# First mixer of a two-layer decoder: where the norm squares, the rotary sum and the decays stand in their engines' order

## The chip, the cores and the metric

The kernel runs on one core of one Trainium2 chip. The metric is device microseconds (us) of one execution; the time before is 1045.48 us, the median of 3 runs that lie between 1041.57 and 1046.89 us.

## The reference

The program is the trunk of a two-layer hybrid decoder on 256 tokens with a model width of 1024. Each layer adds half a SwiGLU feed-forward, a mixer and another half feed-forward to the residual. The mixer of the first layer, the only place that the change touches, joins two kinds of heads that read the same normalized input:

```python
x += 1/2 SwiGLU(RMSNorm(x)); x += W_out[SSD heads | MLA heads](RMSNorm(x)); x += 1/2 SwiGLU(RMSNorm(x))

# MLA heads: low-rank q and kv, RMSNorm on both, rotary part of 32, causal softmax over blocks of 128 rows
p = jax.nn.softmax(where(causal, einsum("bqhd,bkhd->bhqk", q, k) * scale, -inf))
# SSD heads: convolution and SiLU of x, B, C; dt = softplus(...); decays from the cumulated a = dt * A
y_diag = einsum("bclgn,bcsgn,bcgels,bcgesp->bclgep", C, B, exp(segsum(a)), x * dt)
```

The softmax of the MLA heads and the decays exp(segsum(a)) of the SSD heads do not depend on each other. The kernel keeps both at float32 accuracy: it splits every operand into a high and a low part and makes three products of each matrix product.

## The kernel before

All weights come through one stream. For every piece of a weight, `Stream.load` issues a DMA on SyncE into one of 4 raw buffers, has ScalarE cast it to the high part `wh` (L77), and VectorE subtract that to give the low part `wl` (L78). A raw buffer comes free once both have read it. TensorE then multiplies `wh` with the high and the low part of the activations and `wl` with the high part. The pieces are in the order of the program, so a mixer's weights are cast while TensorE still works on what stands before them.

The order in which each engine issues its instructions is made when the program is built: a scheduler takes the program's dependences and a model of durations and lays out a list for each engine. Engines then run their lists in order, so an instruction that waits holds everything behind it on that engine. `order(later, earlier)` adds one more constraint to the scheduler, that `later` stands behind `earlier` in the lists; on one engine it costs no semaphore.

The first mixer, `mixer0` (L461 to L765), runs over two tiles of 128 tokens (t = 0, 1):

- The low-rank products `p_qa` (400 wide: 16 for dt, 384 for q) and `p_kva` (288 wide) go to PSUM. ScalarE squares and sums them into `ssn` (L481, L482, L484) and copies the rotary part of k into `pe` (L483). VectorE adds epsilon (L485), GpSimd takes the power of -1/2 (L234, in `power`), VectorE scales with it into `qn` (L488, L489). TensorE turns `qn` (L117, `m_qaT` and `m_kvT`), and the turned tile is split in high and low again (L229, L230).
- `xbc(c)` makes one of 16 channel tiles of the convolution: 24 matmuls into a PSUM bank (L294 to L296), then `conv_silu`: one ScalarE instruction (L442) and three of VectorE (L444) read the bank, ScalarE's tanh (L447) and a VectorE instruction (L448) finish it. B and C come first (8 tiles), x behind (8 tiles); they are TensorE's work while the rest is prepared. The banks of all projections (`p_xbc`, `p_qb`, `p_kvb`) are 4 in turn.
- The q projection `p_qb` (from L516): for each token tile two halves of 4 heads, 9 matmuls each. ScalarE squares each half (L526) and copies it in two parts (L528, L529), VectorE sums the squares (L527), GpSimd rotates the last 32 columns in five instructions, four products (L457, L458) and their sum (L459), and takes the power for the scale of q (L234 on `sqs`). TensorE turns the result (`m_qT`).
- The kv projection `p_kvb`, with the same steps for k (`knat`, L559 to L564).
- Softplus of dt by `log1p_exp` (L389): ScalarE's Abs (L393) and Exp (L394), a polynomial on VectorE. Its cumulated sum goes to DRAM as `acs_rows` (L592) and comes back spread over all partitions as the E tiles (L648).
- `softmax(t)` (L604): scores on TensorE (`m_sc`), row maximum on VectorE (L617), 8 exponentials of ScalarE with their sums (L622), reciprocal (L419) and, on GpSimd, the product with it (L420); then TensorE turns the probabilities (`m_pT`).
- `decays(t)` (L638): for each of 4 groups of 4 heads 4 Relus (L654) and one Exp (L657) of ScalarE on E, a copy on GpSimd (L659, t = 0 only), and a product with `cb` on VectorE (L660).

What bound the decays to a place in ScalarE's list before is one line: the first Relu of t = 0 stands behind the last tanh of the convolution tiles before it.

Of the kernel before, what the change touches and what calls it, by code (L numbers as in the profile page):

```python
# [11 lines left out]
AF = mybir.ActivationFunctionType  # L12
ALU = mybir.AluOpType
# [43 lines left out]
class Stream:  # L57
# [10 lines left out]
    def load(self, widths):  # L68
        nc = self.nc
        res = []  # L70
        for i, x in enumerate(widths):
            raw = self.pool.tile([P, x], F32, tag="raw", name=f"raw{self.n}_{i}", bufs=self.raw_bufs)
            nc.sync.dma_start(out=raw, in_=self.flat[self.off:self.off + P * x].rearrange("(p w) -> p w", w=x))
            self.off += P * x
            hi = self.pool.tile([P, x], F32R, tag="wh", name=f"wh{self.n}_{i}", bufs=self.bufs)
            lo = self.pool.tile([P, x], F32R, tag="wl", name=f"wl{self.n}_{i}", bufs=self.bufs)
            nc.scalar.copy(out=hi, in_=raw)  # L77
            nc.vector.tensor_tensor(out=lo, in0=raw, in1=hi.bitcast(F32), op=ALU.subtract)  # L78
            res.append((hi, lo))
        self.n += 1  # L80
        return res


class Net:
# [302 lines left out]
        self.proj(NF, at, x, 0.5, after)  # L387


    def log1p_exp(self, v, e, name):  # L390

        nc = self.nc
        nc.scalar.activation(out=e, in_=v, func=AF.Abs)  # L393
        nc.scalar.activation(out=e, in_=e, func=AF.Exp, scale=-1.0)  # L394
        acc = self.blk(list(v.shape), name)
        nc.vector.tensor_scalar(out=acc, in0=e, scalar1=LOG1P[-1], scalar2=None, op0=ALU.mult)
        for c in LOG1P[-2::-1]:
            nc.vector.scalar_tensor_tensor(out=acc, in0=acc, scalar=c, in1=e, op0=ALU.add, op1=ALU.mult)
        return acc
# [50 lines left out]
    def apply_rope(self, out, x, t, which, nh):  # L450

        nc = self.nc
        cg, sg = self.rope[which]
        tmp = self.small([P, nh, 2, 16], f"rtmp{nh}")
        for h in range(2):
            shape = [P, nh, 16]
            nc.gpsimd.tensor_tensor(out=out[:, :, h, :], in0=x[:, :, h, :], in1=cg[:, t, h:h + 1, :].broadcast_to(shape), op=ALU.mult)  # L457
            nc.gpsimd.tensor_tensor(out=tmp[:, :, h, :], in0=x[:, :, 1 - h, :], in1=sg[:, t, h:h + 1, :].broadcast_to(shape), op=ALU.mult)  # L458
        nc.gpsimd.tensor_tensor(out=out, in0=out, in1=tmp, op=ALU.add)  # L459

    def mixer0(self, hT, x, after):  # L461
        nc, st, row = self.nc, self.st, self.row
# [5 lines left out]
        dtv = self.small([P, 2, 16], "dtv")  # L468
# [5 lines left out]
        for t in range(2):  # L474
            c = slice(t * P, (t + 1) * P)
            pq, pk = self.bank([P, 400], "qa"), self.bank([P, 288], "kva")
            self.in_tok(pq, hT, t, w1, 400, 2)
            self.in_tok(pk, hT, t, w2, 288, 2)
            nc.vector.tensor_tensor(out=dtv[:, t, :], in0=pq[:, :16], in1=row[:, ROW["dt_bias"]], op=ALU.add)
            junk = self.small([P, 512], "junk")  # L480
            nc.scalar.activation(out=junk[:, :384], in_=pq[:, 16:], func=AF.Square, scale=384.0 ** -0.5, accum_out=ssn[:, t, 0:1])  # L481
            nc.scalar.activation(out=junk[:, :256], in_=pk[:, :256], func=AF.Square, scale=1.0 / 16, accum_out=ssn[:, t, 1:2])  # L482
            nc.scalar.copy(out=pe[:, t, :], in_=pk[:, 256:])  # L483
            nc.scalar.activation(out=junk[:, :32], in_=pk[:, 256:], func=AF.Square, accum_out=ssn[:, t, 2:3])  # L484
            nc.vector.tensor_scalar(out=ssn[:, t, 0:2], in0=ssn[:, t, 0:2], scalar1=EPS, scalar2=None, op0=ALU.add)  # L485
            self.power(rsn[:, t, :], ssn[:, t, 0:2])
            qn = self.blk([P, 640], "qn", grp="a")
            nc.vector.scalar_tensor_tensor(out=qn[:, :384], in0=pq[:, 16:], scalar=rsn[:, t, 0:1], in1=row[:, ROW["q_a"]], op0=ALU.mult, op1=ALU.mult)  # L488
            nc.vector.scalar_tensor_tensor(out=qn[:, 384:], in0=pk[:, :256], scalar=rsn[:, t, 1:2], in1=row[:, ROW["kv_a"]], op0=ALU.mult, op1=ALU.mult)  # L489
            tp = self.tbank([P, 3, P], "qaT", "a")  # L490
            for j in range(3):
                self.transpose(tp[:, j, :], qn[:, j * P:(j + 1) * P])
            self.split(qaT[0][:, :, c], qaT[1][:, :, c], tp)
            tp = self.tbank([P, 2, P], "kvT", "a")
            for j in range(2):
                self.transpose(tp[:, j, :], qn[:, (3 + j) * P:(4 + j) * P])
            self.split(kvT[:, 0, :, c], kvT[:, 1, :, c], tp)
# [9 lines left out]
        for i in range(4):  # L507
            xbc(8 + i, BC[0][:, i, :])

        wq = st.load([768, 768]) + st.load([768])  # L510
        V = self.blk([P, 2, 8, 64], "V", grp="a")
        qT = [self.blk([96, 8, P], f"qT{t}", grp="a") for t in range(2)]
        kT = [self.blk([96, 8, P], f"kT{t}", grp="a") for t in range(2)]
# [1 line left out]
        for t in range(2):  # L515
            qn = self.blk([P, 8, 96], "qnat", grp="a")  # L516
            qr = self.blk([P, 8, 2, 16], "qr")
            for j in range(2):
                b = self.bank([P, 4, 96], "qb")
                bf = b.rearrange("p a b -> p (a b)")  # L520
                for k in range(3):
                    self.mm_tok(bf, lambda k: (qaT[0][:, k, :], qaT[1][:, k, :]), [k], t,
                                [(wq[k][0][:, j * 384:(j + 1) * 384], wq[k][1][:, j * 384:(j + 1) * 384])], k == 0, k == 2)
                hs = slice(4 * j, 4 * j + 4)
                junk = self.small([P, 512], "junk")[:, :384].rearrange("p (a b) -> p a b", a=4)
                nc.scalar.activation(out=junk, in_=b, func=AF.Square)  # L526
                nc.vector.tensor_reduce(out=sq[:, t, hs], in_=junk, op=ALU.add, axis=X)  # L527
                nc.scalar.copy(out=qn[:, hs, :64], in_=b[:, :, :64])  # L528
                nc.scalar.copy(out=qr[:, hs, :, :], in_=b[:, :, 64:].rearrange("p a (s d) -> p a s d", s=2))  # L529
            self.apply_rope(qn[:, :, 64:].rearrange("p a (s d) -> p a s d", s=2), qr, t, "q", 8)  # L530

            nc.vector.tensor_scalar(out=sq[:, t, :], in0=sq[:, t, :], scalar1=96 * EPS, scalar2=None, op0=ALU.add)
            self.power(sq[:, t, :], sq[:, t, :])
            for j in range(2):
                tp = self.tbank([96, 4, P], "qT", "a")
                for i in range(4):
                    self.transpose(tp[:, i, :], qn[:, 4 * j + i, :])
                nc.scalar.copy(out=qT[t][:, 4 * j:4 * j + 4, :], in_=tp)
# [32 lines left out]


        e = self.small([P, 2, 16], "dte")
        l1 = self.log1p_exp(dtv, e, "dtl")
        dts = self.edge.tile([P, 2, 16], F32, tag="dts", name="dts", bufs=1)
        nc.vector.scalar_tensor_tensor(out=dts, in0=dtv, scalar=0.0, in1=l1, op0=ALU.max, op1=ALU.add)
        ea = self.small([P, 16], "ea")
# [26 lines left out]
        def softmax(t):  # L604
# [3 lines left out]
            for j in range(8 // n):  # L608
# [10 lines left out]
                for i in range(n):  # L619
                    h = n * j + i  # L620
                    m = 8 // (t + 1)
                    nc.scalar.activation(out=pr[h // m][:, h % m, :], in_=b[:, i, :], func=AF.Exp, scale=sq[:, t, h:h + 1],  # L622
                                         bias=mx[:, t, h:h + 1], accum_out=den[:, t, h:h + 1])
                m = 8 // (t + 1)
                h = n * j
                self.normalize(pr[h // m][:, h % m:h % m + n, :], den[:, t, hs])
            for kb in range(t + 1):
                PT[t, kb] = self.turn_probs(lambda h: pr[h // m][:, h % m, kb * P:(kb + 1) * P], kb, f"pT{t}{kb}")
        oT = [self.blk([P, 2, 4, P], f"oT{t}", F32R, grp="a") for t in range(2)]
        for t in range(2):  # L630
            softmax(t)
            self.attend(t, lambda b, h: PT[t, b][:, h, :], lambda b, h: V[:, b, h, :],
                        (oT[t][:, 0], oT[t][:, 1]))

# [3 lines left out]
        def decays(t):  # L638
# [10 lines left out]
            for g in range(4):  # L649
                eb = E[g // 2][:, 4 * (g % 2):4 * (g % 2) + 4, :]  # L650

                for i in range(4):
                    h = t * 16 + 4 * g + i
                    first = nc.scalar.activation(out=eb[:, i, :], in_=eb[:, i, :], func=AF.Relu, scale=-1.0, bias=acs[:, h:h + 1])  # L654
                    if t == g == i == 0:
                        self.order(first, self.tanh)
                nc.scalar.activation(out=eb, in_=eb, func=AF.Exp, scale=-1.0)  # L657
                if t == 0:
                    nc.gpsimd.tensor_copy(out=dec[:, 4 * g:4 * g + 4].unsqueeze(2), in_=eb[:, :, P - 1:P])  # L659
                nc.vector.tensor_tensor(out=eb, in0=eb, in1=cb[:, g:g + 1, :].broadcast_to([P, 4, P]), op=ALU.mult)  # L660
# [504 lines left out]
```

## Time and profile before

| | |
|---|---|
| median of 3 runs | 1045.48 us (1041.57 to 1046.89) |
| the profiled execution | 1043.0 us, span 1041.2 us |
| mean granted TensorE clock | 0.993 |
| TensorE busy (matmul) | 1012.2 us, 97% of the span |
| VectorE, ScalarE, GpSimd busy | 687.4 us (66%), 569.6 us (55%), 86.5 us (8%) |
| DMA | 185.95 MB, mean 179 GB/s |
| chain that ended last | TensorE 92%, ScalarE 2%, DMA 2%, VectorE 2% |

The first mixer lies between about 205 and 333 us of the span. In the profile, a row of a timeline gives the start, the duration, the engine, the line and the operation, output and inputs by the names of the program, how many instructions the row joins, and in brackets the idle time before it with the instruction that ended it. The granted clock of 1.00 is 2.4 GHz, and 0.50 is 1.2 GHz.

### The profile page before, as it was taken

Reading aid. Unit: us, or ns where it says so; the run is one execution under the profiler, and the core shown is the slowest. Engines: PE = TensorE matmul, PEld = TensorE weight load, DVE = VectorE, ACT = ScalarE, POOL = GpSimd, SP = SyncE. Lnnn points to the kernel's source line nnn. Section 1 sums busy time; section 2 is a strip of 40 time slices with the busy share of each in tenths; the row PEclk is TensorE's granted clock in tenths of the full one; section 3 lists DMA queues with packets and bytes.
Section 4 is the critical chain, followed back from the end, with each engine's and each line's share of the span. In section 5 each row is a group of like instructions: output and inputs, shape, how many; then the busy total and the mean of one; then the engine's idle time right before and its main releaser. Section 6 shows DMA issues by size and latency. Waiting matters only on the chain.

```text
span 1041.2 us, 15138 instructions
## 1 busy us (share of the span) xinstructions
PE 1012.2 (97%) x5609; PEld 867.8 (83%) x5609; DVE 687.4 (66%) x1056; ACT 569.6 (55%) x1036; POOL 86.5 (8%) x110
## 2 busy tenths in 40 slices
PE   6999999989799999999999999999999899999998
PEld 5888888888788888888888888888887678888886
DVE  6887654588777667676546776654588576666541
ACT  5665643477767366656434655543466356555530
POOL 2100000006233200000000000000012200000000
PEclk9999999999899999999999999999999899999999
DMA  8875556364434457555564655655463355655451
GB/s 292 273 220 186 190 194 176 116 223 153 158 102 161 144 182 244 194 189 185 198 191 155 229 195 185 194 188 165 142 222 101 103 162 183 190 192 182 150 195 41
DMA packets 52090, 185.95 MB, mean 179 GB/s; under 512 B 5911, under 2 KB 5928, under 8 KB 52016
## 3 DMA queue, kind: packets, MB, share of 16 engines
q1 hardware_dynamic: 49248, 176.58, 51.7%
q0 software_dynamic: 2048, 6.83, 2.0%
q10 hardware_dynamic: 720, 1.57, 0.4%
q8 instruction: 44, 0.72, 0.3%
q14 instruction: 30, 0.25, 0.1%
HBM read 183.89 MB, written 1.06 MB: 178 GB/s over the span
## 4 chain that ended last, share of the span: by engine, by line
PE 92%; ACT 2%; DMA 2%; DVE 2%; issue 1%; POOL 0%; DVEq 0%; ACTq 0%; POOLq 0%
PE p_u L305 13%; PE p_g L305 13%; PE p_acc L322 10%; PE p_acc L321 10%; PE p_acc L323 9%; PE p_u L306 7%; PE p_g L306 7%; PE p_u L279 1%; PE p_u L277 1%; PE p_u L278 1%; PE p_g L277 1%; PE p_g L278 1%; PE p_g L279 1%; PE m_nrm L117 1%; DVE wl L78 1%
## 5 line engine op out<-in xcount | busy, mean ns | idle before, releaser
L78 DVE TENSOR_TENSOR wl<-raw,wh 128x1024 fp32r<-128x1024 f32 (+3 forms) x341 | 414.7, 1226 | 221.0 <-ACT wh L77 217.5
L77 ACT CAST wh<-raw 128x1024 fp32r<-128x1024 f32 (+3 forms) x341 | 351.8, 1039 | 298.1 <-PE p_acc L322 101.5
L305 PE MATMUL p_u<-hT,wh 128*128 128x512 f32 x576 | 204.1, 393 | 0.0
L305 PE MATMUL p_g<-hT,wh 128*128 128x512 f32 x576 | 204.0, 393 | 0.0
L306 PE MATMUL p_u<-hT,wl 128*128 128x256 f32 x576 | 161.7, 281 | 0.0
L306 PE MATMUL p_g<-hT,wl 128*128 128x256 f32 x576 | 161.5, 280 | 0.0
L323 PE MATMUL p_acc<-wl,acth 128*128 128x512 f32 x352 | 137.1, 389 | 0.0
L322 PE MATMUL p_acc<-wh,actl 128*128 128x512 f32 x352 | 137.0, 389 | 0.0
L321 PE MATMUL p_acc<-wh,acth 128*128 128x512 f32 x352 | 136.2, 391 | 0.0
L305 PEld LDWEIGHTS p_g<-hT,wh 128*128 128x128 f32 x576 | 107.9, 187 | 24.5
L305 PEld LDWEIGHTS p_u<-hT,wh 128*128 128x128 f32 x576 | 107.9, 187 | 24.4
L306 PEld LDWEIGHTS p_g<-hT,wl 128*128 128x128 f32 x576 | 108.8, 189 | 0.2
L306 PEld LDWEIGHTS p_u<-hT,wl 128*128 128x128 f32 x576 | 108.8, 189 | 0.0
L323 PEld LDWEIGHTS p_acc<-wl,acth 128*128 128x128 f32 x352 | 66.1, 188 | 13.8
L321 PEld LDWEIGHTS p_acc<-wh,acth 128*128 128x128 f32 x352 | 66.1, 188 | 13.7
L322 PEld LDWEIGHTS p_acc<-wh,actl 128*128 128x128 f32 x352 | 66.1, 188 | 13.3
L234 POOL TENSOR_TENSOR ss<-ss,mhalf 128x1 f32<-128x1 f32 x12 | 6.7, 558 | 578.4 <-DVE ss L252 578.4
L329 DVE SCALAR_TENSOR_TENSOR x<-p_acc,x 128x512 f32<-128x512 f32 x24 | 16.2, 688 | 36.8 <-PE p_acc L323 36.8
L294 PE MATMUL p_xbc<-hT,wh 128*128 128x256 f32 x128 | 37.4, 292 | 0.4 <-DVE cv L444 0.4
L295 PE MATMUL p_xbc<-hT,wh 128*128 128x256 f32 x128 | 37.0, 289 | 0.0
L296 PE MATMUL p_xbc<-hT,wl 128*128 128x256 f32 x128 | 37.0, 289 | 0.0
L381 DVE TENSOR_TENSOR sg<-sg 128x256 f32<-128x256 f32 x72 | 30.6, 425 | 7.9 <-DVE sg L378 0.9
(370 smaller groups left out, 1520.0 us busy)
## 6 DMA issues: line engine op xcount, KB each, us to landing
raw<-in_w SPq DMA_DIRECT2D x326, 512.0 KB, 4.3
gain<-in_gains POOLq DMA_DIRECT2D x5, 512.0 KB, 6.4
E<-acs_rows POOLq DMA_DIRECT2D x4, 512.0 KB, 6.6
raw<-in_w SPq DMA_DIRECT2D x4, 400.0 KB, 3.1
raw<-in_w SPq DMA_DIRECT2D x4, 288.0 KB, 2.9
raw<-in_w SPq DMA_DIRECT2D x3, 384.0 KB, 3.7
raw<-in_w SPq DMA_DIRECT2D x4, 272.0 KB, 2.8
out<-x ACTq DMA_DIRECT2D x4, 256.0 KB, 2.0
```

The source lines that it names most:

```text
L77: nc.scalar.copy(out=hi, in_=raw)
L78: nc.vector.tensor_tensor(out=lo, in0=raw, in1=hi.bitcast(F32), op=ALU.subtract)
L277: mm(out, ah, wh, start=first and i == 0, stop=False)
L294: mm(out, hi[:, cs], xh, start=k == 0, stop=False)
L295: mm(out, hi[:, cs], xl, start=False, stop=False)
L296: mm(out, lo[:, cs], xh, start=False, stop=k == KT - 1)
L305: mm(out, hi[:, cs], hT[k // 2][:, k % 2], start=k == 0, stop=k == KT - 1, skip_group_check=True)
L306: mm(out[:, 0, :], lo[:, cs], self.hk(hT, k)[0], start=False, stop=k == KT - 1, skip_group_check=True)
L321: first = nc.tensor.matmul(o, ah, w[0][:, s], start=k == 0, stop=False)
L322: nc.tensor.matmul(o, al, w[0][:, s], start=False, stop=False)
L323: nc.tensor.matmul(o, ah, w[1][:, s], start=False, stop=k == nk - 1)
L381: nc.vector.tensor_tensor(out=sg, in0=sg, in1=v[:, 1, :], op=ALU.mult)
```

## The change

It makes four additions, all of them to the order that the scheduler has to keep; no instruction is added or taken away. In the diff, lines behind L77 move down by 2 to 9.

- The cast of the first q weight stands behind the last norm square (of t = 1).
- The Abs of softplus stands behind the same square.
- The power for the scale of q stands behind the rotary sum of its tile.
- The first Relu of the decays of a tile t stands behind the last exponential of `softmax(t)`; before, that of t = 0 stood behind a tanh, that of t = 1 was free. Only the first of the 16 Relus of a tile is bound so.

```diff
@@ Stream.load
-            nc.scalar.copy(out=hi, in_=raw)
+            self.cast = nc.scalar.copy(out=hi, in_=raw)
+            if i == 0:
+                self.first = self.cast
@@ log1p_exp(self, v, e, name, behind=None)
-        nc.scalar.activation(out=e, in_=v, func=AF.Abs)
+        first = nc.scalar.activation(out=e, in_=v, func=AF.Abs)
+        if behind is not None:
+            self.order(first, behind)
@@ apply_rope
-        nc.gpsimd.tensor_tensor(out=out, in0=out, in1=tmp, op=ALU.add)
+        return nc.gpsimd.tensor_tensor(out=out, in0=out, in1=tmp, op=ALU.add)
@@ mixer0
-            nc.scalar.activation(out=junk[:, :32], in_=pk[:, 256:], func=AF.Square, accum_out=ssn[:, t, 2:3])
+            squares = nc.scalar.activation(out=junk[:, :32], in_=pk[:, 256:], func=AF.Square, accum_out=ssn[:, t, 2:3])
...
-        wq = st.load([768, 768]) + st.load([768])
+        wq = st.load([768, 768])
+        self.order(st.first, squares)
+        wq += st.load([768])
...
-            self.apply_rope(qn[:, :, 64:].rearrange("p a (s d) -> p a s d", s=2), qr, t, "q", 8)
+            roped = self.apply_rope(qn[:, :, 64:].rearrange("p a (s d) -> p a s d", s=2), qr, t, "q", 8)
...
             self.power(sq[:, t, :], sq[:, t, :])
+            self.order(self.pow, roped)
...
-        l1 = self.log1p_exp(dtv, e, "dtl")
+        l1 = self.log1p_exp(dtv, e, "dtl", squares)
@@ softmax, decays
+                    self.exp = nc.scalar.activation(out=pr[h // m][:, h % m, :], in_=b[:, i, :], func=AF.Exp, ...
...
             softmax(t)
+            exps.append(self.exp)
...
-                    if t == g == i == 0:
-                        self.order(first, self.tanh)
+                    if g == i == 0:
+                        self.order(first, exps[t])
```

ScalarE's list around the norm squares of tile 1 (`qaTh`, `kvT`: turned tile 0; `wh_0_2217`, `wh_1_2223`, `wh_0_2229`: the three q weights; `dte`: softplus), before:

```order
L77 CAST wh_0_2217<-raw_0_2215 128x768
L229 CAST kvT_1912<-m_kvT_1980 128x2x128
L77 CAST wh_1_2223<-raw_1_2221 128x768
L481 ACTIVATE junk_2036,ssn_1908<-p_qa_1985 128x384
L393 ACTIVATE dte_2533<-dtv_1906 128x32
L77 CAST wh_0_2229<-raw_0_2227 128x768
L482 ACTIVATE junk_2036,ssn_1908<-p_kva_1986 128x256
L483 COPY pe_1907<-p_kva_1986 128x32
L394 ACT_TABLE_LOAD
L394 ACTIVATE dte_2533<-dte_2533 128x32
```

And of the changed kernel:

```order
L231 CAST kvT_1912<-m_kvT_1980 128x2x128
L485 ACTIVATE junk_2036,ssn_1908<-p_qa_1985 128x384
L486 ACTIVATE junk_2036,ssn_1908<-p_kva_1986 128x256
L487 COPY pe_1907<-p_kva_1986 128x32
L488 ACTIVATE junk_2036,ssn_1908<-p_kva_1986 128x32
L77 CAST wh_0_2217<-raw_0_2215 128x768
L77 CAST wh_1_2223<-raw_1_2221 128x768
L77 CAST wh_0_2229<-raw_0_2227 128x768
L395 ACTIVATE dte_2533<-dtv_1906 128x32
L446 ACTIVATE cv_2090<-p_xbc_2065,conv_140 128x256
```

The squares moved ahead of three casts, the Abs and the table load; the first convolution tile (`cv_2090`) moved ahead of the table load too.

GpSimd's list at the rotary part of q, tile 0 (`qnat`: q, `sqs`: the scale of q), before:

```order
L458 TENSOR_TENSOR rtmp_180_2271<-qr_2240,sgq_199 128x8x16
L457 TENSOR_TENSOR qnat_2239<-qr_2240,cgq_198 128x8x16
L458 TENSOR_TENSOR rtmp_180_2271<-qr_2240,sgq_199 128x8x16
L234 TENSOR_TENSOR sqs_2238<-sqs_2238,mhalf_81 128x8
L459 TENSOR_TENSOR qnat_2239<-qnat_2239,rtmp_180_2271 128x8x32
```

And of the changed kernel:

```order
L462 TENSOR_TENSOR rtmp_180_2271<-qr_2240,sgq_199 128x8x16
L461 TENSOR_TENSOR qnat_2239<-qr_2240,cgq_198 128x8x16
L462 TENSOR_TENSOR rtmp_180_2271<-qr_2240,sgq_199 128x8x16
L463 TENSOR_TENSOR qnat_2239<-qnat_2239,rtmp_180_2271 128x8x32
L236 TENSOR_TENSOR sqs_2238<-sqs_2238,mhalf_81 128x8
```

The power and the rotary sum changed places.

ScalarE's list around the softmax of tile 0 (`E_266`, `E_267`: E of heads 0 to 7 and 8 to 15; `p_237`: probabilities; `cv`, `cth`: convolution tiles), before:

```order
L654 ACTIVATE E_267_2812<-E_267_2812,acs_2555 128x128 x8
L77 CAST wh_1_3256<-raw_1_3254 128x1024
L657 ACTIVATE E_266_2811<-E_266_2811 128x512
L447 ACTIVATE cth_2884<-cv_2879 128x256
L442 ACTIVATE cv_2918<-p_xbc_2893,conv_140 128x256
L77 CAST wh_0_3262<-raw_0_3260 128x1024
L442 ACTIVATE cv_2957<-p_xbc_2932,conv_140 128x256
L657 ACTIVATE E_267_2812<-E_267_2812 128x512 x2
L622 ACTIVATE p_237_2649,den_2645<-m_sc_2650,mx_2646,sqs_2238 128x128 x4
L77 CAST wh_1_3268<-raw_1_3266 128x1024
L442 ACTIVATE cv_2996<-p_xbc_2971,conv_140 128x256
L622 ACTIVATE p_237_2649,den_2645<-m_sc_2665,mx_2646,sqs_2238 128x128 x4
```

And of the changed kernel:

```order
L663 ACTIVATE E_266_2811<-E_266_2811,acs_2555 128x128 x7
L451 ACTIVATE cth_2642<-cv_2637 128x256
L663 ACTIVATE E_267_2812<-E_267_2812,acs_2555 128x128 x8
L446 ACTIVATE cv_2918<-p_xbc_2893,conv_140 128x256
L77 CAST wh_1_3256<-raw_1_3254 128x1024
L451 ACTIVATE cth_2884<-cv_2879 128x256
L666 ACTIVATE E_266_2811<-E_266_2811 128x512
L666 ACTIVATE E_267_2812<-E_267_2812 128x512
L629 ACTIVATE p_237_2649,den_2645<-m_sc_2650,mx_2646,sqs_2238 128x128 x4
L629 ACTIVATE p_237_2649,den_2645<-m_sc_2665,mx_2646,sqs_2238 128x128 x4
L663 ACTIVATE E_266_2811<-E_266_2811,acs_2555 128x128
L666 ACTIVATE E_267_2812<-E_267_2812 128x512
```

The 8 exponentials now stand together, ahead of one Relu and two of the four Exps of the decays; 15 Relus and the other two Exps still stand ahead of them, with two weight casts and two convolution instructions fewer than before.

## Rows read from the trace of the kernel before

**Rows 1.** The page, part 1: busy time of each engine.

```profile
PE 1012.2 (97%) x5609; PEld 867.8 (83%) x5609; DVE 687.4 (66%) x1056; ACT 569.6 (55%) x1036; POOL 86.5 (8%) x110
```

**Rows 2.** Waits of TensorE, 170 to 420 us: total, times, longest.

```profile
PE m_pT L117 <- POOL p L420: 5.4, 1, 5.4
PE m_qaT L117 <- DVE qn L488: 3.1, 1, 3.1
...
PE m_qT L117 <- POOL qnat L459: 0.5, 1, 0.5
PE p_xbc L294 <- DVE cv L444: 0.4, 1, 0.4
```

**Rows 3.** Timeline of TensorE at the turn of tile 1's norm.

```profile
219.81 0.28 PE L296 MATMUL p_xbc<-hT,wl 128*128 128x256 f32 x1
223.21 0.52 PE L117 MATMUL m_qaT<-sq,qn 128*128 128x128 f32 x3 [3.12 <-DVE qn L488]
```

**Rows 4.** Timeline of ScalarE, 214 to 220 us.

```profile
214.36 0.37 ACT L229 CAST kvT<-m_kvT 128x256 fp32r<-128x256 f32 x1
...
217.62 0.38 ACT L482 ACTIVATE junk<-p_kva 128x256 f32<-128x256 f32 x1
...
218.18 1.28 ACT L394 ACT_TABLE_LOAD   x1
```

**Rows 5.** Timeline of VectorE, 220 to 223 us.

```profile
220.37 1.00 DVE L444 SCALAR_TENSOR_TENSOR cv<-p_xbc,conv,cv 128x255 f32<-128x255 f32 x2 [1.56 <-ACT cv L442]
...
222.45 0.61 DVE L488 SCALAR_TENSOR_TENSOR qn<-p_qa,rsn,row 128x384 f32<-128x384 f32 x1
```

**Rows 6.** Timeline of GpSimd, 218 to 283 us.

```profile
218.93 0.70 POOL L234 TENSOR_TENSOR rsn<-ssn,mhalf 128x2 f32<-128x2 f32 x1
...
236.28 2.62 POOL L234 TENSOR_TENSOR sqs<-sqs,mhalf 128x8 f32<-128x8 f32 x1
...
257.92 1.12 POOL L648 DMA_DIRECT2D E<-acs_rows  x2 [0.49 <-DMA acs_rows<-acsT]
259.04 1.03 POOL L564 TENSOR_TENSOR knat<-pr,rk 128x256 f32<-128x256 f32 x1
...
281.36 1.04 POOL L420 TENSOR_TENSOR p<-p,rden 128x512 f32<-128x512 f32 x1 [2.77 <-DVE rden L419]
```

**Rows 7.** Timeline of TensorE at the turn of the probabilities, 282 to 289 us.

```profile
282.45 1.12 PE L117 MATMUL m_pT<-sq,p 128*128 128x128 f32 x4 [5.41 <-POOL p L420]
283.93 0.58 PE L294 MATMUL p_xbc<-hT,wh 128*128 128x256 f32 x1 [0.35 <-DVE cv L444]
...
286.66 0.33 PE L294 MATMUL p_xbc<-hT,wh 128*128 128x256 f32 x1
...
288.50 0.60 PE L117 MATMUL m_pT<-sq,p 128*128 128x128 f32 x4
```

**Rows 8.** Timeline of ScalarE, 264 to 280 us.

```profile
264.14 2.16 ACT L654 ACTIVATE E<-E,acs 128x128 f32<-128x128 f32 x7 [4.11 <-DMA E<-acs_rows]
...
270.17 2.44 ACT L654 ACTIVATE E<-E,acs 128x128 f32<-128x128 f32 x8
...
276.14 1.14 ACT L657 ACTIVATE E<-E 128x512 f32<-128x512 f32 x2
277.18 0.45 ACT L622 ACTIVATE p<-m_sc,mx,sqs 128x128 f32<-128x128 f32 x1
...
278.92 1.05 ACT L77 CAST wh<-raw 128x1024 fp32r<-128x1024 f32 x1
```

**Rows 9.** Busy by stretch: PE, PEld, DVE, ACT, POOL, granted clock, DMA share, GB/s.

```profile
277.00:283.00 6.00, 0.59 (x4) 0.55 (x4) 6.00 (x10) 6.00 (x20) 2.63 (x3) 0.74 0.33 117
283.00:290.00 7.00, 6.64 (x45) 5.91 (x44) 6.95 (x15) 2.84 (x8) 1.93 (x1) 0.73 0.46 151
```

**Rows 10.** Timeline of ScalarE behind the first half of the q projection.

```profile
231.32 0.48 ACT L526 ACTIVATE junk<-p_qb 128x384 f32<-128x384 f32 x1
...
231.95 0.29 ACT L529 COPY qr<-p_qb 128x128 f32<-128x128 f32 x1
```

More of the change, by code (lines that the diff above doesn't have):

```diff
@@ L387, in ffn, with log1p_exp @@
         self.proj(NF, at, x, 0.5, after)
-    def log1p_exp(self, v, e, name):
+    def log1p_exp(self, v, e, name, behind=None):
         nc = self.nc
-        nc.scalar.activation(out=e, in_=v, func=AF.Abs)
+        first = nc.scalar.activation(out=e, in_=v, func=AF.Abs)
+        if behind is not None:
+            self.order(first, behind)
         nc.scalar.activation(out=e, in_=e, func=AF.Exp, scale=-1.0)
@@ L621, in softmax @@
                     m = 8 // (t + 1)
-                    nc.scalar.activation(out=pr[h // m][:, h % m, :], in_=b[:, i, :], func=AF.Exp, scale=sq[:, t, h:h + 1],
-                                         bias=mx[:, t, h:h + 1], accum_out=den[:, t, h:h + 1])
+                    self.exp = nc.scalar.activation(out=pr[h // m][:, h % m, :], in_=b[:, i, :], func=AF.Exp, scale=sq[:, t, h:h + 1],
+                                                    bias=mx[:, t, h:h + 1], accum_out=den[:, t, h:h + 1])
                 m = 8 // (t + 1)
@@ L629, in mixer0 @@
         oT = [self.blk([P, 2, 4, P], f"oT{t}", F32R, grp="a") for t in range(2)]
+        exps = []
         for t in range(2):
             softmax(t)
+            exps.append(self.exp)
             self.attend(t, lambda b, h: PT[t, b][:, h, :], lambda b, h: V[:, b, h, :],
```

## The prediction

> **What bounds the kernel now.** I read the page first: TensorE is busy for 1012.2 us, 97% of the span [rows 1], so only what lets TensorE idle, or run slowly, can move the time. Then the waits of TensorE around the first mixer: a wait of 5.4 us in front of the turned probabilities `m_pT`, for the GpSimd product L420; one of 3.1 us in front of `m_qaT`, for VectorE's L488; 0.5 us in front of `m_qT`, for the rotary sum L459; 0.4 us in front of a convolution tile, for a bank that L444 had not left [rows 2]. Last the timelines of the releasing engines, for why each was late.
>
> - *The norm.* TensorE ends its convolution tile just after 219.81 and stands until 223.21 [rows 3]. ScalarE's squares of this tile could begin at 214.7, when `kvT` is done, but stand behind casts and softplus: the second begins at 217.62, and the first convolution instruction only after a table load of 1.28 us [rows 4]. VectorE waits 1.56 us for that convolution instruction, and L488 stands behind it, at 222.45 [rows 5], though its power began at 218.93 [rows 6]. So it is ScalarE's list, felt through VectorE's list.
> - *The rotation.* The power on `sqs` takes 2.62 us of GpSimd at 236.28, and the sum that TensorE waits for stands behind it [rows 6].
> - *The probabilities.* E lands and frees ScalarE at 264.14; 15 Relus (2.16 us for 7, 2.44 for 8), two late Exps (1.14 us) and other work stand ahead of the first exponential at 277.18 [rows 8]. The product for the first 4 heads ends at 282.40 [rows 6], and TensorE goes on at 282.45 after 5.41 us [rows 7].
>
> **A clock that fell.** Over 277 to 283 us the granted clock averages 0.74, over 283 to 290 us 0.73 [rows 9]. As a mix of 1.00 and 0.50 that is 0.52 x 6 + 0.54 x 7 = 6.9 us at 1.2 GHz. What it cost is read from matmuls: 12 of them take 2.73 us, from 283.93 to 286.66, where the next 15 take 1.84, or 0.123 each (1.5 for 12), and the turn takes 1.12 instead of 0.60 [rows 7]: 1.26 + 0.52, or 1.8 us. The rest of the slow stretch lay in the idle time.
>
> The Trainium skill, TensorE: Matmul & The Clock Gate, section Terms, prices throttled time at its length times the share of the clock that is taken; that would be 3.4 us here (an estimate from that page), and the sum below 1.6 us lower. The rows speak against it in this stretch, since no matmul ran in its first part.
>
> **The change, part by part.**
>
> *Squares ahead of casts, softplus behind them.* No work is added. In the new list the four instructions on the norm directly follow `kvT`: the second square and the copy take 0.56 together (217.62 to 218.18 [rows 4]); for the first, half as wide again, I take 0.5, for the small last one 0.2, so they run from 214.7 to 216.0. Epsilon and the power of 0.70 us [rows 6] then end near 216.7, about when the first delayed q cast ends; one subtraction of VectorE (under 1 us) stands in between, and L488, of 0.61 us [rows 5], would end near 218.2. TensorE's idle time began at 220.1 (223.21 less 3.12 [rows 3]): the wait goes, with a margin of nearly 2 us. The casts move back by some 2 us. Their cover is that the first half of `p_qb`, which needs them, ended at 231.3 [rows 10]; even 3.12 sooner that is about 10 us behind the last of the casts. The raw buffers that they hold come free as much later, so SyncE's next loads do too; that I price at 0, covered by the same stretch. If the cover were gone, each us would be paid in full. What moved behind is the table load, now past the first convolution instruction. **-3.12.**
>
> *Rotary sum ahead of the power.* The sum no longer stands behind 2.62 us; the power's result is only wanted by the softmax, 40 us later. **-0.47**; that is all the 0.5 us wait can give.
>
> *Decays behind the softmax.* Read literally it would put 16 Relus and 4 Exps behind the exponentials. The list shows that it holds only the first Relu: 15 Relus and two Exps still stand ahead. What goes from before the exponentials is the other two Exps, 1.14 us [rows 8], two casts of about 1 us and two convolution instructions; and the 8 exponentials stand together. Walking the new list from E's landing: 7 Relus 2.16, 8 Relus 2.44, two tanh, one convolution instruction and one cast 2.1 (the cast 1.05 [rows 8], the others shorter), two Exps 1.14, four exponentials 1.74 (277.18 to 278.92), reciprocal and product 1.2 [rows 6, 8]: the probabilities of the first heads are ready 10.7 us after E, where before it took 18.3 (264.14 to 282.40). E itself moves too: its two DMAs now stand behind `knat`, 1.03 us [rows 6], on GpSimd's queue, whose wait for `acs_rows` covers about half; so E lands 0.5 us later against what precedes it. TensorE's turn moved back by 17 matmuls, 2 us. Ready is then 7 us earlier, wanted 2 us later, against a wait of 5.41: a margin of about 3 us. **-5.41**, and with it the bank wait of **-0.35** behind it and the clock, **-1.8**. The delayed Exps and Relu feed VectorE's product with `cb` and the scan 25 us later, and are priced at 0.
>
> *What becomes late next.* Three terms, which no wait of before shows.
> - The second half of q tile 0 now reuses the bank of the first half, so it must wait until L526 to L529 have read it: from 231.32 to 232.24 [rows 10], where before the second half started as the first ended. With the hand-over **+1.2**; between 0.9 (these rows alone) and 1.6 (if a tanh that stands ahead of it in ScalarE's list is late).
> - VectorE and ScalarE were busy 6.00 of 6.00 us while TensorE idled, and VectorE 6.95 of the next 7 [rows 9]. Without that idle time the convolution tiles come to VectorE 5.4 us sooner. Walking its new list, the bank for the second convolution tile behind the probabilities comes free about 1 us after TensorE wants it. **+1.0**; between 0 and 3.6, the idle time that the first two edits remove and could hand on to here. I take the walk, since the evacuations ahead of the exponentials also come earlier.
> - The turned output of tile 1 stands nearer to the end of the output projection; its split into two parts, the size of what rows 10 show, may stand bare: **+0.6**, between 0 and 1.2.
>
> Sum: 3.12 + 0.47 + 5.41 + 0.35 + 1.8 = 11.15 off, 2.8 on, **8.35 us faster**. The profiled execution took 1043.0, which gives 1034.7; the median shown stands 2.5 us above it, which gives 1037.1. I forecast the middle, **1036**. Half a per cent, 5.2 us, is about what a measurement of this kernel can tell from no change: faster means under 1040.3.
>
> **The rivals.**
>
> *The first gains are given back (0.17).* Removing 3.6 us at the norm and the rotation brings TensorE that much sooner to a stretch where VectorE has no slack; four banks let it run ahead, but the 0.35 us wait for L444 came even after 5.41 us of standing still [rows 7]. Against it: that wait stood behind products with `cb` that the new list puts elsewhere. Gain 4.8: about 1039.5, on either side of the bound alike.
>
> *It does not do what it says (0.16).* 15 Relus and two Exps ahead of the softmax remain, and if ScalarE's and VectorE's lists run later than I walked, the `m_pT` wait returns with its slow clock. Then 7.56 of the 11.15 stays; less the 2.8, 0.8 us is left of the gain: about 1043.
>
> *The new waits are absorbed (0.10).* Banks come free early, since evacuation stands sooner in the lists: 11.15 us, about 1033.
>
> *Slower (0.09).* One mechanism: ScalarE's list keeps the softmax, and the evacuation of a convolution tile (`cv_2918`), behind 15 Relus that wait for E. If E comes late, ScalarE stands, banks stay full, and TensorE stops on convolution tiles as well as on `m_pT`. Each us beyond the margin of 3 is paid in full. E took 6.2 us from its issue to 264.14 [rows 6, 8]; 11 us more than that eats the whole 8.35, and 17 more gives 1036 + 14 = 1050. For it speaks that the E DMAs moved behind `knat` on GpSimd's queue; against it that only half a us of this is bare.
>
> **How the numbers follow.** The forecast has 0.48, and its own range, from the bounds of the three new terms, is 1034 to 1039. Faster: 0.48 + half of 0.17 + 0.10 = 0.67. Within half a per cent: the other half and 0.16, 0.24. Slower: 0.09. For 8 times in 10 the range runs from 1031.5, below the third rival by the scatter of the runs, to 1043; it leaves out the slower case and part of the second rival.
>
> **What would show it.** Right: no wait of TensorE for L488's successor (L492) and none over 1 us for the probabilities; a granted clock of 1.00 from 277 to 290 us; a new wait of about 1 us of `p_qb` for the ScalarE copy L535. Wrong: a wait of `m_pT` of over 2 us, a `p_xbc` that waits over 2 us in sum for L448 (L444 before), or the E Relus starting more than 3 us later against TensorE's work than before.

## The result and the profile after

The changed kernel takes 1034.12 us (median of 4 runs, 1033.59 to 1034.71), against 1045.62 us before in the same session (1041.57 to 1046.89): a ratio of 0.9897, with a 95% interval of 0.9882 to 0.9912. The profiled execution has a span of 1032.6 us, 8.6 less than before. All of it lies in the first mixer, whose output projection reaches beyond the 333 us named ahead: TensorE begins the next feed-forward at 366.66 us instead of 375.31. First the row of before, then that of the changed kernel:

```profile
375.31 0.39 PE L277 MATMUL p_g<-wh,hT 128*128 128x512 f32 x1
```

```profile
366.66 0.39 PE L279 MATMUL p_g<-wh,hT 128*128 128x512 f32 x1
```

TensorE's waits of the changed kernel over the same stretch, 170 to 420 us (total, times, longest), to be held against [rows 2]:

```profile
PE p_qb L279 <- ACT qr L535: 1.0, 1, 1.0
PE p_xbc L296 <- DVE cv L448: 0.8, 1, 0.8
PE p_kvb L279 <- ACT qr L535: 0.7, 1, 0.7
PE m_acs L590 <- DVE a L587: 0.5, 1, 0.5
PE p_acc L323 <- ACT yT L231: 0.4, 1, 0.4
```

The waits of 5.4, 3.1 and 0.5 us are gone. Three new ones stand where the prediction put them: 1.0 for the q bank (1.2 forecast), 0.8 for a convolution bank (1.0), 0.4 for the turned output (0.6). The 0.5 us of `m_acs` was not forecast: the cumulated sum of softplus, whose Abs moved back, now comes just late (the wait also stands in the runs e1 and e6 below, which have that edit, and not in e5, which doesn't).

The norm in the changed kernel, ScalarE's timeline, against [rows 4]:

```profile
214.41 0.49 ACT L485 ACTIVATE junk<-p_qa 128x384 f32<-128x384 f32 x1 [0.46 <-DVE dtv L483]
...
215.53 0.20 ACT L488 ACTIVATE junk<-p_kva 128x32 f32<-128x32 f32 x1
...
215.72 2.29 ACT L77 CAST wh<-raw 128x768 fp32r<-128x768 f32 x3
...
218.04 0.56 ACT L446 ACTIVATE cv<-p_xbc,conv 128x256 f32<-128x256 f32 x1
...
219.73 1.28 ACT L398 ACT_TABLE_LOAD   x1
```

VectorE's and TensorE's rows of the same place, against [rows 3, 5]:

```profile
217.53 0.61 DVE L492 SCALAR_TENSOR_TENSOR qn<-p_qa,rsn,row 128x384 f32<-128x384 f32 x1
```

```profile
220.30 0.49 PE L119 MATMUL m_qaT<-sq,qn 128*128 128x128 f32 x3
```

The squares end at 215.7 (216.0 forecast), L492 at 218.1 (218.2), and TensorE comes to `m_qaT` at 220.30 without waiting: a margin of 2.2 us (nearly 2).

The softmax of tile 0, ScalarE's timeline, against [rows 8]:

```profile
262.69 2.16 ACT L663 ACTIVATE E<-E,acs 128x128 f32<-128x128 f32 x7 [0.46 <-DMA E<-acs_rows]
...
265.06 2.43 ACT L663 ACTIVATE E<-E,acs 128x128 f32<-128x128 f32 x8
...
269.10 1.14 ACT L666 ACTIVATE E<-E 128x512 f32<-128x512 f32 x2
270.15 0.45 ACT L629 ACTIVATE p<-m_sc,mx,sqs 128x128 f32<-128x128 f32 x1
```

The product on GpSimd and the turn on TensorE, against [rows 6, 7]:

```profile
272.74 1.04 POOL L424 TENSOR_TENSOR p<-p,rden 128x512 f32<-128x512 f32 x1 [1.78 <-DVE rden L423]
```

```profile
276.49 0.60 PE L119 MATMUL m_pT<-sq,p 128*128 128x128 f32 x4
...
279.36 0.35 PE L296 MATMUL p_xbc<-hT,wh 128*128 128x256 f32 x1 [0.79 <-DVE cv L448]
```

The probabilities are ready at 273.78, 11.1 us after E (10.7 forecast, 18.3 before); TensorE wants them at 276.49, a margin of 2.7 (3). The granted clock stays at 1.00 where it averaged 0.74 and 0.73 [rows 9]; after the clock, the columns are DMA share and GB/s:

```profile
277.00:283.00 6.00, 5.21 (x49) 4.87 (x50) 6.00 (x10) 4.94 (x8) 0.19 (x1) 1.00 0.42 132
283.00:290.00 7.00, 7.00 (x61) 6.57 (x58) 7.00 (x13) 4.70 (x9) 0.80 (x1) 1.00 0.79 257
```

### The profile page after: what moved, and what is told of

Read it like the earlier page. It is cut to its first block, busy times and chain, and to the rows that moved or that the text cites. A ratio compares the mean times of both kernels' runs of the same rounds, so it can differ in the third digit from the quotient of the medians.

```text
span 1032.6 us, 15136 instructions
## 1 busy us (share of the span) xinstructions
PE 1011.2 (98%) x5609; PEld 866.7 (84%) x5609; DVE 686.0 (66%) x1056; ACT 568.6 (55%) x1036; POOL 83.8 (8%) x110
## 4 chain that ended last, share of the span: by engine, by line
PE 93%; ACT 2%; DMA 2%; DVE 2%; issue 1%; POOL 1%; DVEq 0%; POOLq 0%; ACTq 0%
PE p_u L307 13%; PE p_g L307 13%; PE p_acc L324 10%; PE p_acc L323 10%; PE p_acc L325 10%; PE p_u L308 7%; PE p_g L308 7%; PE p_u L281 1%; PE p_u L280 1%; PE p_u L279 1%; PE p_g L279 1%; PE p_g L280 1%; PE p_g L281 1%; PE m_nrm L119 1%; DVE wl L80 1%
## 5 line engine op out<-in xcount | busy, mean ns | idle before, releaser
L77 ACT CAST wh<-raw 128x1024 fp32r<-128x1024 f32 (+3 forms) x341 | 351.5, 1039 | 297.6 <-PE p_acc L324 102.3
L325 PEld LDWEIGHTS p_acc<-wl,acth 128*128 128x128 f32 x352 | 66.1, 188 | 13.8
```

Source lines behind the costliest of these rows:

```text
L77: self.cast = nc.scalar.copy(out=hi, in_=raw)
L325: nc.tensor.matmul(o, ah, w[1][:, s], start=False, stop=k == nk - 1)
```

## The experiments

The walk through the lists held. What it did not test is which edit makes which piece of the list. The scheduler lays out all engines anew from every constraint, so a list that differs at the softmax need not come from the edit at the softmax.

**One edit at a time.** `e1_norm_only` keeps the two constraints on the norm and takes the other two edits back:

```diff
-            self.order(self.pow, roped)
-                    if g == i == 0:
-                        self.order(first, exps[t])
+                    if t == g == i == 0:
+                        self.order(first, self.tanh)
```

> Only the first cast and the Abs behind the norm squares; rotary and decays as before. Theory A, each edit removes its own wait (as the prediction's sum has it): the 3.1 us wait for L488 goes, about 1.2 us of a p_qb bank wait comes, the m_pT wait of 5.4 us stays with its slow clock: 1043 to 1044. Theory B, the norm's edit also makes the scheduler lay out the softmax anew (in this kernel's ScalarE list the 8 exponentials stand together behind 15 Relus and only two of the four Exps, with no decays edit at all): no m_pT wait, 1034 to 1036, m_qT still waiting 0.5 us.

Measured: 1037.5 us against 1045.1, a ratio of 0.9929 (0.9905 to 0.9952). TensorE's waits, 205 to 345 us:

```profile
PE m_att_o L416 <- ACT pT L437: 1.8, 1, 1.8
PE p_qb L279 <- ACT qr L535: 1.0, 1, 1.0
PE p_kvb L279 <- ACT qr L535: 0.7, 1, 0.7
PE m_acs L589 <- DVE a L586: 0.6, 1, 0.6
PE p_xbc L296 <- DVE cv L448: 0.5, 1, 0.5
```

Neither `m_qaT` nor `m_pT` waits: theory B, though a wait of 1.8 us for the evacuation of the turned probabilities keeps it 1.5 to 3.5 us above what it said. `m_qT` doesn't wait either, without the rotary edit.

`e2_rope_only` keeps only `self.order(self.pow, roped)`.

> Only the power of q's scale behind the rotary sum. Both theories: only GpSimd's list changes, m_qT no longer waits 0.5 us, all else as before: 1045.1, 0.5 us faster than before, within the scatter. If a later wait takes the 0.5 us up, no change at all and the m_pT wait 0.5 us longer.

Measured: 1045.38 us, a ratio of 0.9996 (0.9981 to 1.0011). The `m_qT` wait is gone, the time is that of before. Half a us is within what this measurement can't tell.

Its profile shows something else. Apart from the power and the sum that change places on GpSimd, its lists are those of before, yet TensorE waits 3.8 us for the probabilities instead of 5.4. E landed 4.9 us behind the start of its issue here, and 6.2 before [rows 6, 8]:

```profile
256.65 1.11 POOL L656 DMA_DIRECT2D E<-acs_rows  x2
```

```profile
261.57 2.16 ACT L662 ACTIVATE E<-E,acs 128x128 f32<-128x128 f32 x7 [2.40 <-DMA E<-acs_rows]
```

```profile
279.89 1.12 PE L119 MATMUL m_pT<-sq,p 128*128 128x128 f32 x4 [3.79 <-POOL p L424]
```

The turn begins 18.3 us behind E's landing in both (279.89 less 261.57; 282.45 less 264.14 [rows 7, 8]). So in this list, by these profiles, each us by which E lands later is a us of TensorE's. In the change the margin of 2.7 us stands between the two.

`e3_decays_only` keeps only the new place of the first Relu.

> Only the first Relu of a tile's decays behind that tile's last exponential. Theory A: the m_pT wait of 5.4 us, 0.35 us and the slow clock's 1.8 us go, 1.0 us of bank waits comes: 1039. Theory B: in this kernel's ScalarE list one Relu and one Exp (0.9 us) fewer stand ahead of the exponentials, and the scores stand as late as before: the m_pT wait shrinks by about 1 us and keeps its slow clock, the 3.1 us wait stays: 1044 to 1045.

Measured: 1044.84 us, a ratio of 0.9991 (0.9975 to 1.0007). Its waits in the mixer begin:

```profile
PE m_pT L119 <- POOL p L424: 5.8, 1, 5.8
PE m_qaT L119 <- DVE qn L492: 3.3, 1, 3.3
```

Theory A is off by nearly 6 us. Theory B's time is right, its smaller wait not: one Relu and one Exp fewer ahead of the exponentials did not make the probabilities earlier for TensorE. The edit that names the softmax does nothing for it alone.

`e5_cast_only` keeps one line, `self.order(st.first, squares)`.

> Only the first q cast behind the norm squares; softplus, rotary and decays as before. The squares then still stand ahead of all three casts, but ScalarE's list at the softmax is that of before (15 or 16 Relus and all four Exps ahead of the exponentials). If the norm's wait and the softmax's place are two separate gains: the 3.1 us wait for L488 goes, a p_qb bank wait of about 1 us comes, the m_pT wait and its slow clock stay: 1043. If the norm's 3.1 us were the cause of all that the first run gained: 1037.5. If what the norm gives is only handed on to m_pT: 1045 and an m_pT wait of 8 us.

Measured: 1042.81 us, a ratio of 0.9971 (0.9959 to 0.9983).

```profile
PE m_pT L119 <- POOL p L424: 5.4, 1, 5.4
PE p_qb L279 <- DVE cv L448: 1.0, 1, 1.0
...
PE m_sc L619 <- ACT kT L576: 0.6, 1, 0.6
PE m_qT L119 <- POOL qnat L463: 0.6, 1, 0.6
```

This is the norm's wait by itself: it goes, waits of 1.0 and 0.6 us come, the softmax stays as it was. So the norm and the softmax are two gains. The first comes with the cast, by the runs (10 against 29). Its profiled execution doesn't show it: the span of 1042.2 us is 1.0 longer than that of before. E landed 7.5 us behind its issue (256.18 to 263.69), and the turn again stands 18.3 us behind that, at 282.00, only 0.45 ahead of before. Behind the turn 21 convolution matmuls run 0.21 us apart, where before there were 12 [rows 7], which takes about 0.8 more. In the lists as built, not all of which were run, the cast edit alone, and the cast left out of the change, both keep the softmax's exponentials in two groups; the cast with softplus (e1), or with the rotary edit, brings them together. The decays edit makes no difference to that.

`e6_no_rope` is the change without the rotary edit.

> The change without the rotary edit; TensorE's, ScalarE's and VectorE's lists are those of the change, only the power and the rotary sum stand the other way round on GpSimd. If the rotary edit is worth its 0.5 us in the sum: 1034.6, with m_qT waiting about 0.5 us. If it is worth nothing, because other work of TensorE now stands ahead of m_qT: 1034.1, the time of the change.

Measured: 1033.01 us (1032.70 to 1033.71), a ratio of 0.9882 (0.9865 to 0.9898), whose interval overlaps the change's. Its GpSimd and TensorE rows:

```profile
233.90 1.64 POOL L236 TENSOR_TENSOR sqs<-sqs,mhalf 128x8 f32<-128x8 f32 x1
235.51 0.73 POOL L463 TENSOR_TENSOR qnat<-qnat,rtmp 128x256 f32<-128x256 f32 x1
```

```profile
238.15 1.04 PE L119 MATMUL m_qT<-sq,qnat 128*96 128x128 f32 x8
```

With the power ahead of it, the sum still ends 1.9 us before TensorE comes: the two instructions took 2.4 us here and 4.3 before, and TensorE comes later by the new q bank wait. The rotary edit adds nothing to the change.

**The softmax's place without the norm.** `e4_all_relus` holds every Relu in the changed kernel; `e7_relus_t0` holds the 16 of tile 0 in the kernel before.

```diff
-                    if g == i == 0:
+                    if True:      # e4_all_relus, in the change
+                    if t == 0:    # e7_relus_t0, with the norm and rotary edits taken back
```

> The change with every Relu of a tile's decays behind the softmax, not the first alone. If the probabilities' margin is what counts (they are ready 2.7 us before TensorE wants them in the changed kernel), nothing more is to be had there: within 1 us of the changed kernel, 1033.5 to 1035, with ScalarE no longer waiting for E ahead of the softmax. Rival: the decays, now 5 us later, hold the products with cb and the scan (m_yd waits), 1 to 5 us slower than the changed kernel.

> Norm and rotary as before; all 16 Relus of tile 0 behind its softmax, tile 1 free. If the softmax's place in ScalarE's list is what pays: the m_pT wait and the slow clock go without any norm edit, the 3.1 us wait for L488 stays: 1038 to 1039. If, as with all Relus in the change, the late products with cb hold the gates and the output projection (3.1 us and a slower clock): 1041 to 1043. If the place pays only together with the norm: 1045.

Measured: 1039.83 us for e4 (ratio 0.9953, 0.9935 to 0.9970) and 1044.29 us for e7 (0.9993, 0.9982 to 1.0004). The largest wait of each in the mixer:

```profile
PE p_acc L323 <- DVE gate L716: 3.1, 1, 3.1
```

```profile
PE p_acc L323 <- DVE gate L714: 3.3, 1, 3.3
```

In both the `m_pT` wait is gone from the mixer, and the output projection waits instead, for VectorE's gates; the clock over 290 to 333 us falls to 0.92 and 0.95. In e4 VectorE has four products with `cb` (2.50 us) right ahead of the gates. For e4 the rival was right, in another place than it named and by more than its 1 to 5 us (5.7 between the medians of two sessions). So the change's weak constraint, which holds one Relu of 16, is worth more than the literal one. e7 has the time of its third case and the waits of its second: taking the `m_pT` wait away is no gain in itself, the list behind it must fit too.

**What the clock costs.** `e8_fill` takes no wait away; it gives TensorE something to do in one.

```diff
+            if j == 0 and fill is not None:
+                for i in range(18):
+                    d = self.nc.tensor.matmul(tp, self.identb, self.mask[:, P:]..., start=True, stop=True)
```

> The kernel before with 18 added matmuls (mask times identity, written to the bank that the turned probabilities overwrite) at the place where TensorE waits for the probabilities: the wait's length stays, most of it is filled with work. By the prediction's rows the slow clock cost 1.8 us there: granted clock 1.00 from 277 to 290 us, about 1043.3. By the length of the slow stretch times the share taken, 3.4 us: 1041.7. If the clock does not hang on the idle time: no gain and still a stretch near 0.5, 1045.

Measured: 1044.32 us, a ratio of 0.9989 (0.9976 to 1.0002): the interval (2.5 us faster to 0.2 slower) holds both 1.8 us and nothing, though not 3.4, so the profile must decide between the first two. Its granted clock in three stretches:

```profile
222.00:229.00 7.00, 5.47 (x26) 5.50 (x27) 6.02 (x10) 2.82 (x6) 0.00 (x0) 0.51 0.68 210
...
277.00:283.00 6.00, 4.02 (x30) 3.13 (x29) 6.00 (x12) 6.00 (x16) 2.20 (x3) 1.00 0.49 160
283.00:290.00 7.00, 6.64 (x46) 5.03 (x45) 7.00 (x14) 4.26 (x14) 2.97 (x2) 1.00 0.35 100
```

Filled, the place keeps its clock. TensorE's rows there, before and then in e8:

```profile
276.67 0.38 PE L117 MATMUL m_xsT<-sq,xT 128*128 128x128 f32 x2
```

```profile
279.30 0.38 PE L117 MATMUL m_xsT<-sq,xT 128*128 128x128 f32 x2
281.66 4.05 PE L430 MATMUL m_pT<-mask,identb 128*128 128x512 bf16 x18 [1.98 <-ACT p L627]
285.54 0.60 PE L117 MATMUL m_pT<-sq,p 128*128 128x128 f32 x4
...
288.04 0.28 PE L294 MATMUL p_xbc<-hT,wh 128*128 128x256 f32 x1
```

From the start of `m_xsT` to the 13th convolution matmul behind the turn it takes 8.7 us (279.30 to 288.04), where before it took 10.0 (276.67 to 286.66 [rows 7]): 1.25 us saved. The turn itself began 0.5 us later against `m_xsT`, because the added matmuls run on past the end of the product for which it waits (284.98). Without that 0.5, which the filling costs, the clock is worth 1.7 us, against the 1.8 of the prediction. The Trainium skill (TensorE: Matmul & The Clock Gate, section Terms) would have made it an estimated 3.4, and the measurement decides against it here.

The first row was the surprise: 0.51 after the norm's idle time, which in the profile of before had left the clock at 1.00:

```profile
222.00:229.00 7.00, 5.79 (x49) 5.82 (x50) 7.00 (x12) 4.32 (x8) 0.00 (x0) 1.00 0.69 225
```

In e8, 19 convolution matmuls start between 224.06 and 228.04 us, 0.21 us apart for the most part instead of 0.12. The turns of the norm that stand around them, before (with 223.21 in [rows 3]) and then in e8:

```profile
225.83 0.38 PE L117 MATMUL m_kvT<-sq,qn 128*128 128x128 f32 x2
```

```profile
223.53 0.87 PE L117 MATMUL m_qaT<-sq,qn 128*128 128x128 f32 x3 [3.32 <-DVE qn L493]
...
228.25 0.63 PE L117 MATMUL m_kvT<-sq,qn 128*128 128x128 f32 x2
```

From one to the other it is 2.6 us before and 4.7 in e8 for the same matmuls: here the slow clock costs 2.1 us. `e3_decays_only` shows 0.76 in the stretch from 222 to 229 us. So `e9_fill2` also fills the norm's wait, with 12 matmuls.

> The kernel before with the 18 added matmuls of the run e8_fill at the probabilities and 12 more (384 wide, written to the bank that the turned q overwrites) at the place where TensorE waits 3.1 us for the norm; no wait is taken away. Theory C: the idle time at the norm lowers the clock in some executions and not in others (1.00 in the profile of before, 0.51 over 222 to 229 us in that of e8_fill), and this is most of the scatter of the kernel before (1042.2 to 1049.1 us): with both places filled the runs lie within about 2 us of each other, with a median of 1042 to 1043, and the granted clock is 1.00 through the mixer. Rival: the scatter has another source: it stays at 5 us or more, the median 1043 to 1045.

Measured: 1042.1 us, a ratio of 0.9959 (0.9945 to 0.9973), with runs from 1040.3 to 1042.8. The kernel before, in that session, ran from 1043.3 to 1047.5.

```profile
222.00:229.00 7.00, 5.95 (x50) 5.83 (x50) 7.00 (x13) 4.77 (x9) 0.00 (x0) 1.00 0.70 224
```

Theory C's signs are there, with a little more spread than its 2 us: with its waits kept, but filled, the kernel gains 4.3 us (2.8 to 5.8) and its 6 runs spread over 2.5 us, where 11 of before spread over 4.2. The added matmuls do no useful work; what they buy is the clock: the mean granted clock of these runs is 0.995 to 0.998, that of before in the session 0.990 to 0.993. The runs of before alone say the same. Of the 29 in the session of e8, the nine with the lowest mean clock, 0.990, took 1046.5 to 1049.1 us, and the two with the highest, 0.995, took 1042.2 and 1042.6.

**A bank for the new wait.** `e10_bank` gives the second half of q's tile 0 a bank of the transposes' pair; `e11_bank_no_rope` is the same without the rotary edit.

```diff
-                b = self.bank([P, 4, 96], "qb")
+                b = self.sbank([P, 4, 96], "qb", "a") if (t, j) == (0, 1) else self.bank([P, 4, 96], "qb")
```

> The change with the second half of q's tile 0 in a PSUM bank of the transposes' pair instead of the four of the projections, so that it needn't wait for the first half to be read. If the new wait of 1.0 us is worth its size: 1033, 1.1 us faster than the change, no p_qb wait for the copy L535. Rival: the scheduler lays out the rest anew and another bank or transpose waits in its place: 1034 or more.

> The same as e10_bank without the rotary edit. If the rotary edit is worth nothing once the norm's list is changed, within 0.7 us of e10_bank; if its 0.5 us stands, e10_bank is faster by that and m_qT waits here; if it costs (the run without it measured 1 us below the change), this one is about 1 us faster than e10_bank.

Measured, in one session: 1035.45 us (0.9899, 0.9884 to 0.9914) and 1036.70 us (0.9916, 0.9900 to 0.9933). The new wait is gone, and another is there, 2.8 us in e10 and 2.7 in e11:

```profile
PE m_qT L119 <- POOL qnat L463: 2.8, 1, 2.8
```

The rival was right: by its ratio e10 is as fast as the change (0.9897), and the q tile waits for the next thing instead, longer, while other waits have gone. Of the three cases for e11 none came as stated: by the medians it is 1.25 us slower than e10, with the same wait, and the intervals overlap. The profiles, e10's and then e11's, differ by the clock behind that wait:

```profile
240.00:244.00 4.00, 4.00 (x25) 3.55 (x24) 3.97 (x12) 2.92 (x10) 2.56 (x6) 1.00 0.70 238
```

```profile
240.00:244.00 4.00, 4.00 (x15) 3.22 (x14) 3.85 (x14) 2.37 (x8) 2.65 (x6) 0.65 0.58 201
```

From `m_qT` to the 12th matmul of `p_kvb` behind it e10 takes 3.45 us and e11 5.0. That is 1.6 of the 1.8 us between their spans, so these two show no price of the rotary edit. No version here beats the change by more than these measurements can tell.

## Why the prediction was right, and where it wasn't

- **The forecast**, 1036 us in a range of 1031.5 to 1043, faster by 8.35 us on the profiled execution: the spans differ by 8.6, the medians by 11.5. The forecast case came. The total could be right with wrong shares (below), because the lists that were walked were those of the whole change.
- **The norm, -3.12:** right. The list, the times of each step and the margin came within 0.3 us of the walk.
- **The step that failed** is the one headed "Decays behind the softmax". Its -5.41, -0.35 and -1.8 are there in the profile, but they are not that edit's: alone its ratio of 0.9991 can't be told from none (e3), while the norm edits without it remove the `m_pT` wait (e1). I read the lists of the whole change and gave each difference to the edit that stands nearest in the code. What the decays edit does, on top of the norm edits, is spare the 1.8 us wait of `m_att_o` that e1 shows and e6 doesn't.
- **The rotary sum, -0.47:** mis-assigned. It removes its wait alone (e2), but in the change there is none to remove (e6).
- **The clock, -1.8:** right at its place (1.7, e8); much of the slow stretch was idle anyway and cost nothing more. What the sum lacked is the clock at the norm: a slow stretch there cost 2.1 us in e8. The profiled execution of before showed none, so I priced none; other executions have it. The medians differ by 2.9 us more than the profiled spans, and e9, with both waits filled, gains 2.5 us more than the 1.8 of the one place: the sizes fit, within wide intervals.
- **The new waits, +2.8:** 1.0 + 0.8 + 0.4, and 0.5 at a place not named: 2.7. The 0.6 of `p_kvb` for `knat`, which I left standing, went.
- **The rivals.** The first gains were not given back, and the new waits were not absorbed. "It does not do what it says" was true of the cause and not of the time. For the slower case, E came at 262.69, 1.5 us sooner than before [rows 8] and 6.2 us behind its issue as before. Against TensorE's work it came about 1 us later: TensorE reached the place of `m_pT` 12.9 us behind E before and 13.8 in the change, where that place had moved back by 2. That is short of the 3 us that the prediction named as a sign of being wrong.

Not settled: why the scheduler moves the softmax when two of the constraints meet, and whether the rotary edit costs anything (e6 measured below the change, e11 above e10, the latter with a slower clock).

## What to carry to other kernels

Where a scheduler lays out the engines' lists, read the new lists for the time, but give no edit its share before building it alone: here the two constraints on the norm together made the softmax's gain, and the edit on the softmax made none by itself. A constraint that is stronger in the sense of its own purpose can be worse (all Relus against one), since what it pushes back comes out further down, here ahead of the gates. And look at the spread of the runs, and at the mean granted clock of each, before pricing an idle place of TensorE: one that lowers the clock in some executions shows there, when one profile doesn't.

## What the runs showed of the hardware that was not expected

- An idle time of 3.1 to 3.3 us in the same place left the granted clock at 1.00 in one execution (before, 3.12 us), at 0.76 over 7 us in another (e3, 3.3 us), and at 0.51 in a third (e8, 3.3 us). A wait of 2.75 us in front of `m_qT` left it at 1.00 in e10 and at 0.65 over 4 us in e11. Kernels that keep the norm's wait spread over 3.5 to 7 us in their runs (before: 1042.2 to 1049.1 in 29 runs), and e11 over 3.8 in 6; the change, with neither, spreads over 1.1 in 4.
- The mean clock does not account for all of the scatter. The ten runs of e5, which keeps only the wait of 5.4 us at the probabilities, spread over 4.3 us, and the mean clock of each is 0.993. One candidate is E, which landed 4.9 to 7.5 us behind the start of its issue in the profiles in which ScalarE stands waiting for it (e2 the shortest, e5 the longest) and there sets when TensorE goes on. Another is where the slow stretch lies: by the same mean clock it held 12 matmuls behind the turn before and 21 in e5. No run tries either alone.
- GpSimd's power of 128x8 took 2.62 us before and in the change, and 1.64 in e6 for the same tile; its sum of 128x256 took 1.73, 1.72 and 0.73. What runs beside them on the other engines makes this difference or not: no run tried it.
